# x read feature-major, and twelve pairs' C11 products first, the early ones on inputs that are not normalized

## The chip, the cores and the metric

One Trainium2 chip, one of its cores. The metric is the device time of one execution in microseconds; the median of three runs of the kernel before is 1115.58 us (1115.43 to 1116.25).

## The reference

A two-layer decoder trunk over 1024 tokens of width 1024, all in float32. Layer 0: `y = rms_norm(x)`, one projection `proj = y @ w_in` to 6144 columns, split into u (pooled with trailing windows 2, 4, 8, 16, then mixed by `w_pool`), gate_b, gate_c and h_c (the gated width-3 convolution `gate_b * conv(gate_c * h_c)`), and z (2048 columns, SiLU gate over both), then `@ w_out` and the residual. Layer 1: `rms_norm`, a q/k/v/gate projection, sliding-window attention with sinks and partial rotary, gate, `@ w_o`, residual. A final rms_norm.

```python
def rms_norm(x, g):
    x32 = x.astype(jnp.float32)
    r = x32 * lax.rsqrt(jnp.mean(x32 * x32, axis=-1, keepdims=True) + NORM_EPS)
    return (r * g.astype(jnp.float32)).astype(x.dtype)
```

The factor of a token is the rsqrt; `g` is a factor of the feature.

## The kernel before

Everything lies feature-major: 128 features on the partitions, 512 tokens (half of the sequence, s = 0 or 1) along a row. Float32 accuracy comes from splitting each operand into a high part, which ScalarE rounds to fp32r (`cast`, L181 or L469), and a low part, which VectorE gets by subtracting the high part from the source (`low`, L182 or L472). A product of two operands is then three matmuls (high x high, high x low, low x high).

The projections use Strassen's scheme in Winograd's form on 2 x 2 blocks: weights are taken in pairs of 128-column blocks, the 1024 features in two halves of 512 and the tokens in two halves. A pair needs seven products instead of eight, each of four feature slices times three matmuls of 512 columns (12 matmuls, L388). Their names are those of the weight side: A11 and A12 (a first block's feature halves, times B11 and B21, which are the normalized inputs of the first 512 tokens), S2, S1, S3, A22 and S4 (sums of weight blocks, times T2, T1, T3, T4 and B22, which are sums or parts of the normalized inputs). The sum of A11 B11 and A12 B21 is the output block C11. Layer 0 has 24 pairs: four U (pooled channels), eight CH (gate_c and h_c), eight BZ (gate_b and z), four Z (z of the pooled half), worked off as U, CH, BZ, Z, CH, BZ for each quarter of the channels; layer 1 has 9.

`Strassen.prods` is the list of all products in the order in which their weights are prepared. `prepare_to(n)` splits the weights of the next products (a cast on ScalarE, a low part on VectorE, three VectorE sums ahead of S2) and issues later loads from SyncE's queue; `lead` is 3, so weights are ready three products ahead. Weight tiles come from the pool `W` with 9 slots of 4 KB. `go_ahead` runs the A11 and A12 products of the first AHEAD = 6 pairs before any pair is worked off as a whole: B11 and B21 are all that they need, and while TensorE does them, VectorE and ScalarE make T1 to T4 and B22 (the `combine`, `cast` and `low` steps handed to it). After each product ScalarE copies the PSUM bank out, and a store puts it into `c_dram`; `pair` loads it back later and does the other five products (`pair` does all seven for the other pairs, L409).

The opening (L533 to L602) stands in an order written out by hand on TensorE, ScalarE, VectorE and SyncE (`order()`). x is read token-major, eight tiles of 128 tokens x 1024 features (`load_x`, 512 KB each). ScalarE squares a tile and sums along the row (`square`, L542); after four tiles `rsqrt_mean` (L129) gives the tokens' factors; VectorE multiplies by the factor and by `g` (`normed`, L545); TensorE transposes 128 x 128 blocks (`turned`, L553), and the results are copied out to Y. Then B11 and B21 are split, the first product starts, four products run, the second half is transposed, and eight more follow. Warm-up matmuls (L529) run in the first microseconds and between the transposes. From `ordered.close()` on only TensorE's order is the program's; the other engines are ordered by the scheduler.

Layer 1 uses the same class with all nine pairs ahead (AHEAD1 = 9). Its column sums (`col_sums`, L176) and its factor rows (`diag_r` L153 to L164, `spread_r` L166: a diagonal of the factors, multiplied by ones, gives a row of factors on all partitions) are the functions that the change also uses in layer 0.

Of the kernel before, what the change touches and what calls it, by code (L numbers as in the profile page):

```python
# [18 lines left out]
P = 128  # L19
# [17 lines left out]
AHEAD = 6  # L37
AHEAD1 = 9
# [35 lines left out]
def trunk(ctx, tc, x, xT, g1, pos, cols, w_in, w_pool, w_out, w_l1, b_kv, sinks, w_o, g_fin, out):  # L74
# [10 lines left out]
    c_dram = tc.dram_tile([AHEAD, 2, P, HALF], F32, name="c_dram")  # L85
    o_dram = tc.dram_tile([16, 2, P, HALF], F32, name="o_dram")
    c1_dram = tc.dram_tile([AHEAD1, 2, P, HALF], F32, name="c1_dram")
# [224 lines left out]
    class Strassen:  # L312


        def __init__(self, src, pairs, first, c_dram, bank, s1, u2, keep0):
            self.src, self.pairs, self.first, self.c_dram = src, pairs, first, c_dram
            self.bank, self.s1, self.u2, self.keep0 = bank, s1, u2, keep0
            pr = [(i, n) for j in range(0, first, 2) for n in ("A11", "A12")
                  for i in range(j, min(j + 2, first))]
            pr += [(i, n) for i in range(first) for n in order_ if n not in ("A11", "A12")]  # L320
            pr += [(i, n) for i in range(first, len(pairs)) for n in order_]
            if keep0 is False:
                for i in range(first - 1):
                    pr.remove((i, "S4"))
                    pr.insert(pr.index((i + 1, "S2")) + 1, (i, "S4"))
# [3 lines left out]
            self.kept, self.c_bank, self.ahead = {}, {}, {}  # L329
            self.store, self.rest, self.defer = nc.sync.dma_start, None, False  # L330
# [5 lines left out]
        def load_for(self, n):  # L336

            if n < len(self.prods):
                i, what = self.prods[n]
                if what == "A11":  # L340
                    self.load_w(i, 0)
                if i < self.first and what == "S2":
                    self.load_w(i, 0)
                    self.load_w(i, 1)

        def prepare_to(self, n):
            while self.prepared < min(n, len(self.prods)):
# [5 lines left out]
                a11, a12 = wraw[i, 0][:, 0:4], wraw[i, 0][:, 4:8]  # L353
                if not ahead:
                    if (i, 1) not in wraw:
# [10 lines left out]
                src = a11 if what in ("A11", "S2") else a12 if what in ("A12", "S4") else \  # L366
# [24 lines left out]
        def go_ahead(self, *steps):  # L391
# [984 lines left out]
```

## Time and profile before

| what | value |
|---|---|
| median of three runs | 1115.58 us |
| the profiled execution | 1114.73 us, span 1112.9 us |
| TensorE busy | 1060.9 us, 95% of the span, 4780 matmuls |
| VectorE busy | 816.7 us, 73% |
| ScalarE busy | 502.6 us, 45% |
| granted TensorE clock, mean | 0.987 |
| moved by DMA | 143.7 MB, mean 129 GB/s |

Busy time is time in which an engine has an instruction under way. A matmul that is part of a stream is listed at some 395 ns, though the next begins 233 ns behind it, so starts are what is to be compared. [...]

### The profile page before, as it was taken

The page shows a single profiled execution, that of the slowest core. Times are in us where ns is not written, and L with a number is a line of the kernel's source. Part 1 is how long each engine was busy: PE and PEld are TensorE (multiplying, and loading weights), DVE is VectorE, ACT ScalarE, POOL GpSimd, SP SyncE. Part 2 cuts the span into 40 slices and gives each one's busy share as a digit, 9 for nine tenths or more (in the row PEclk, how much of TensorE's full clock was granted, in tenths as well). Part 3 has the DMA queues.
Part 4 walks back from the last instruction along what each step waited for, and adds up shares of the span by engine and source line. Part 5 has one row for each costly group of instructions (what it writes and reads, how often), then busy time and mean ns, then how long its engine had stood idle before and what let it go on. Part 6 is the DMA issues. An engine that isn't in the chain of part 4 may idle for free. (4 is left out here: it accounts for less than half of the span.)

```text
span 1112.9 us, 13964 instructions
## 1 busy us (share of the span) xinstructions
PE 1060.9 (95%) x4780; PEld 860.5 (77%) x4780; DVE 816.7 (73%) x1544; ACT 502.6 (45%) x1007; POOL 124.1 (11%) x204
## 2 busy tenths in 40 slices
PE   3999999999999999999999999999989988999997
PEld 3778788888888888888788888877867776788886
DVE  4699979967697578955744784397688777888874
ACT  4753342333224231432633653264244698766652
POOL 0000000000000000000000000003120021455552
PEclk9999999999999999999999999999989999999999
DMA  5343331131211221224544553355348836756451
GB/s 209 107 170 102 133 129 57 67 113 39 76 57 67 95 76 38 95 86 154 204 172 142 199 174 119 122 180 180 114 160 274 276 115 178 209 115 124 97 103 39
DMA packets 108136, 143.71 MB, mean 129 GB/s; under 512 B 39584, under 2 KB 64288, under 8 KB 108064
## 3 DMA queue, kind: packets, MB, share of 16 engines
q1 hardware_dynamic: 99856, 126.03, 36.0%
q10 hardware_dynamic: 8208, 16.78, 4.1%
q8 instruction: 38, 0.62, 0.2%
q14 instruction: 34, 0.28, 0.1%
HBM read 106.35 MB, written 36.44 MB: 128 GB/s over the span
## 5 line engine op out<-in xcount | busy, mean ns | idle before, releaser
L181 ACT CAST W<-W 128x512 fp32r<-128x512 f32 (+1 forms) x234 | 156.4, 679 | 284.6 <-DVE W L363 101.3
L182 DVE TENSOR_TENSOR W<-W 128x512 fp32r<-128x512 f32 (+1 forms) x234 | 175.4, 759 | 110.8 <-ACT W L181 69.7
L388 PE MATMUL b<-U,W 128*128 128x512 f32 x432 | 110.9, 410 | 5.1 <-DVE t L433 2.2
L388 PEld LDWEIGHTS b<-U,W 128*128 128x128 f32 x432 | 82.6, 196 | 24.3 <-ACT W L181 2.7
L388 PE MATMUL b<-B11h,W 128*128 128x512 f32 x264 | 88.9, 401 | 2.7 <-ACT W L181 1.8
L388 PE MATMUL b<-B22h,W 128*128 128x512 f32 x264 | 88.5, 396 | 2.1 <-DVE t L442 2.0
L388 PE MATMUL b<-B21h,W 128*128 128x512 f32 x264 | 87.6, 396 | 1.3 <-ACT W L400 1.3
L388 PE MATMUL b<-T2h,W 128*128 128x512 f32 x192 | 65.5, 402 | 1.9 <-ACT W L181 1.9
L388 PE MATMUL b<-T3h,W 128*128 128x512 f32 x192 | 64.2, 395 | 0.0
L388 PE MATMUL b<-T1h,W 128*128 128x512 f32 x192 | 64.2, 395 | 0.0
L388 PE MATMUL b<-T4h,W 128*128 128x512 f32 x192 | 63.2, 390 | 0.0
L388 PEld LDWEIGHTS b<-B11h,W 128*128 128x128 f32 x264 | 50.3, 191 | 15.7 <-ACT W L181 2.3
L388 PEld LDWEIGHTS b<-B22h,W 128*128 128x128 f32 x264 | 49.5, 188 | 15.2 <-ACT t L987 2.0
L388 PEld LDWEIGHTS b<-B21h,W 128*128 128x128 f32 x264 | 49.6, 188 | 13.8 <-ACT W L400 2.1
L1102 ACT ACTIVATE pt<-psB,smax 128x128 f32<-128x128 f32 x128 | 45.7, 366 | 20.8 <-DVE smax L1100 20.2
L828 PE MATMUL psD<-U,W 128*128 128x512 f32 x128 | 51.3, 401 | 2.6 <-DVE U L182 2.6
L388 PE MATMUL b<-B11l,W 128*128 128x512 f32 x132 | 52.8, 400 | 0.8 <-DVE B11l L472 0.8
L388 PE MATMUL b<-B21l,W 128*128 128x512 f32 x132 | 52.1, 395 | 0.0
L388 PE MATMUL b<-B22l,W 128*128 128x512 f32 x132 | 52.1, 394 | 0.0
L1225 PE MATMUL b<-U,aH 128*128 128x512 f32 (+1 forms) x128 | 49.8, 389 | 1.6 <-DVE U L182 1.6
L829 PE MATMUL psD<-U,W 128*128 128x512 f32 x128 | 51.1, 400 | 0.0
L827 PE MATMUL psD<-U,W 128*128 128x512 f32 x128 | 51.1, 399 | 0.0
(286 smaller groups left out, 2476.2 us busy)
## 6 DMA issues: line engine op xcount, KB each, us to landing
W<-w_in SPq DMA_DIRECT2D x54, 512.0 KB, 3.3
W<-w_out SPq DMA_DIRECT2D x32, 512.0 KB, 3.4
W<-w_l SPq DMA_DIRECT2D x27, 512.0 KB, 3.9
t<-q_dram SPq DMA_DIRECT2D x32, 256.0 KB, 4.3
o_dram<-t SPq DMA_DIRECT2D x30, 256.0 KB, 2.0
t<-c_dram SPq DMA_DIRECT2D x28, 256.0 KB, 3.8
c_dram<-W ACTq DMA_DIRECT2D x18, 256.0 KB, 3.2
T<-xT SPq DMA_DIRECT2D x16, 256.0 KB, 4.2
```

The costliest lines, as they stand in the source:

```text
L181: nc.scalar.copy(out=dst_h, in_=src)
L182: sub(out=dst_l, in0=src, in1=dst_h.bitcast(F32), op=ALU.subtract)
L388: mm(dst, lhsT=w[:, hw, k], rhs=x[hx][:, k], start=start and k + n == 0, stop=k == 3 and n == 2, skip_group_check=not start)
L827: mm(dst, lhsT=w[k][0], rhs=oHL[f][0], start=(f == 0), stop=False)
L828: mm(dst, lhsT=w[k][0], rhs=oHL[f][1], start=False, stop=False)
L829: mm(dst, lhsT=w[k][1], rhs=oHL[f][0], start=False, stop=(f == 15))
L1102: act(out=res[g][:, 2 * i2 + i, :], in_=bv[:, i, P:256], func=AF.Exp, scale=0.125, bias=smax[:, at + i:at + i + 1], accum_out=den[:, at + ...
L1225: mm(o, lhsT=a[0][:, kk, :], rhs=woL[8 * n + k][:, c], start=False, stop=False)
```

## The change

x is no longer read token-major: `xT` (feature-major) is loaded in sixteen slices of 128 features x 512 tokens (256 KB) straight into Y, and the tile of `g` on all partitions, the 64 transposes and their copies out of PSUM go. Each slice of the first half is multiplied by `g` (a factor per partition here) and split into G11 and G21, operands that lack the tokens' factors (they use the space of T1 and B22). The first twelve products, A11 of six pairs and then A12 of the same six, run on G11 and G21. Since a token is a column of the product, its factor is applied afterwards: VectorE multiplies the PSUM bank by a row of factors on its way to SBUF (`scaled`), in place of ScalarE's copy, and SyncE stores it to `c_dram`. The sums of squares come from squares of the slices (VectorE for the first half, ScalarE for the second) and small matmuls with two columns of ones (`stat`, four per slice); `root` and `spread` make the rows. Then x itself is normalized in Y (`normed`), B11 and B21 are split as before, and twelve more products, of six further pairs, run on them while T1 to T4 and B22 are made. So twelve pairs instead of six are ahead: the eight BZ and the four Z (`early`). They were U0, CH0, BZ0, CH1, BZ1 and Z0.

The weights of the products ahead are loaded in halves of 256 KB, just the part that is needed, and `load_ahead` keeps `look` of them on their way. Copies of products ahead lie in tiles of their own. In `pair`, an early pair does S3 in front of S1. Layer 1 takes the same class, with the same nine pairs in the same groups as before.

The calls of the schedule are written several to a line here.

```diff
-AHEAD = 6
-AHEAD1 = 9
+GROUPS = (6, 2, 2, 2)
+GROUPS1 = (2, 2, 2, 2, 1)
...
-        def __init__(self, src, pairs, first, c_dram, bank, s1, u2, keep0):
+        def __init__(self, src, pairs, early, groups, c_dram, bank, s1, u2, defer):
+            first = len(early)
             self.src, self.pairs, self.first, self.c_dram = src, pairs, first, c_dram
-            self.bank, self.s1, self.u2, self.keep0 = bank, s1, u2, keep0
-            pr = [(i, n) for j in range(0, first, 2) for n in ("A11", "A12")
-                  for i in range(j, min(j + 2, first))]
-            pr += [(i, n) for i in range(first) for n in order_ if n not in ("A11", "A12")]
-            pr += [(i, n) for i in range(first, len(pairs)) for n in order_]
-            if keep0 is False:
-                for i in range(first - 1):
+            self.bank, self.s1, self.u2, self.early = bank, s1, u2, early
+            pr, j = [], 0
+            for n_ in groups:
+                pr += [(i, n) for n in ("A11", "A12") for i in early[j:j + n_]]
+                j += n_
+            pr += [(i, n) for i in range(len(pairs))
+                   for n in (("S2", "S3", "S1", "A22", "S4") if i in early else order_)]
+            if defer:
+                for i in range(len(pairs) - 1):
                     pr.remove((i, "S4"))
                     pr.insert(pr.index((i + 1, "S2")) + 1, (i, "S4"))
...
-                if what == "A11":
+                if n < 2 * self.first:
+                    k = 4 * int(what == "A12")
+                    self.part[i, what] = W([P, 4, P])
+                    nc.sync.dma_start(out=self.part[i, what],
+                                      in_=self.src[self.pairs[i][0]][:, k:k + 4])
+                elif what == "A11":
                     self.load_w(i, 0)
-                if i < self.first and what == "S2":
+                if i in self.early and what == "S2":
                     self.load_w(i, 0)
                     self.load_w(i, 1)
+
+        def load_ahead(self, n):
+            while len(self.loaded) < min(n, 2 * self.first):
+                self.loaded.append(self.load_for(len(self.loaded)))
 
...
+                src = self.part.pop((i, what)) if ahead else a11 if what in ("A11", "S2") else a12 if what in ("A12", "S4") else \
...
-                    if at_ + 2 < 2 * self.first:
-                        self.load_for(at_ + 2)
-                    elif at_ + 1 == 2 * self.first:
+                    self.load_ahead(at_ + 1 + self.look)
+                    if at_ + 1 == 2 * self.first:
                         self.load_for(2 * self.first)
                 elif i + 1 < len(self.pairs):
-                    if what == "A12" or i < self.first and what == "S3":
+                    if what == "A12" or i in self.early and what == "S1":
                         self.load_w(i + 1, 0)
                     if what == "A22":
...
+        def go_ahead(self, *steps, names=("B11", "B21"), row=None, late=None):
...
-                    self.c_bank[i], self.kept[i] = self.bank(), W([P, 2, HALF])
-                self.product(self.c_bank[i], i, what, ("B11", "B21")[j], j == 0)
-                t = self.kept[i][:, j]
-                nc.scalar.copy(out=t, in_=self.c_bank[i])
-                if i or not self.keep0:
-                    self.store(out=self.c_dram[i, j], in_=t)
-                    t = self.c_dram[i, j]
-                self.ahead[i, j] = t
-                self.prepare_to(min(len(self.ahead) + LEAD, 2 * self.first + 3))
+                    self.c_bank[i] = self.bank()
+                self.ahead[i, j] = None
+                self.product(self.c_bank[i], i, what, names[j], j == 0)
+
+                def rest(i=i, j=j, row=row):
+                    t = self.out()
+                    if row is None and late is None:
+                        nc.scalar.copy(out=t, in_=self.c_bank[i])
+                    else:
+                        tt(out=t, in0=self.c_bank[i], in1=row(), op=ALU.mult)
+                    self.ahead[i, j] = at_ = self.c_dram[self.early.index(i), j]
+                    self.store(out=at_, in_=t)
+
+                if late is None:
+                    rest()
+                else:
+                    late.append(rest)
+                self.prepare_to(min(len(self.ahead) + self.lead, 2 * self.first + 3))
...
+            if i in self.early:
+                p1, c = t3(), t3()
+                for j, t in enumerate((p1, c)):
+                    nc.sync.dma_start(out=t, in_=self.ahead[i, j])
                 c11(c)
             else:
                 p1 = t3()
@@ -433,15 +453,21 @@
             tt(out=u2_, in0=b2, in1=p1, op=ALU.add)
             self.finish_pair()
             run(0)
+            if i in self.early:
+                b2 = bank()
+                product(b2, i, "S3", "T3")
+                tt(out=p1, in0=b2, in1=u2_, op=ALU.add)
+                run(1)
             b3 = bank()
             product(b3, i, "S1", "T1")
-            run(1)
-            b2 = bank()
-            product(b2, i, "S3", "T3")
-            tt(out=p1, in0=b2, in1=u2_, op=ALU.add)
+            if i not in self.early:
+                run(1)
+                b2 = bank()
+                product(b2, i, "S3", "T3")
+                tt(out=p1, in0=b2, in1=u2_, op=ALU.add)
             tt(out=o22, in0=b3, in1=p1, op=ALU.add)
             run(2)
-            if i >= self.first:
+            if i not in self.early:
                 product(b1, i, "A12", "B21", False)
                 c11(b1)
...
+    st0 = Strassen(w_in, pairs, [BZ[j] for j in range(8)] + [Z[g] for g in range(4)], GROUPS,
+                   c_dram, bank,
...
+    ops["G11"], ops["G21"] = ops["T1"], ops["B22"]
...
+    def xt(s, k):
+        return Y[f"{k // 4 + 1}{s + 1}"][:, k % 4]
+    def load_x(s, *ks):
+        for k in ks:
+            nc.sync.dma_start(out=xt(s, k), in_=xT[k * P:(k + 1) * P, hs(s)])
+    def operand(k):
+        h, lo = (t[:, k % 4] for t in ops[("G11", "G21")[k // 4]])
+        act(out=h, in_=xt(0, k), func=AF.Copy, scale=col(C_G1, k))
+        stt(out=lo, in0=xt(0, k), scalar=col(C_G1, k), in1=h.bitcast(F32), op0=ALU.mult,
+            op1=ALU.subtract)
+    sq, sums, rows = {}, {}, {}
+    def square(s, k):
+        sq[s, k] = xp.tile([P, HALF], F32, name="sq", bufs=4)
+        if s:
+            act(out=sq[s, k], in_=xt(s, k), func=AF.Square)
+        else:
+            tt(out=sq[s, k], in0=xt(s, k), in1=xt(s, k), op=ALU.mult)
+    def stat(s, k):
+        if k == 0:
+            sums[s] = bank()
+        for b in range(4):
+            c = 8 * k + 2 * b
+            mm(sums[s][:, c:c + 2], lhsT=sq[s, k][:, b * P:(b + 1) * P], rhs=ones[:, 0:2],
+               start=True, stop=True)
+    def root(s):
+        r = rcol0[:, 4 * s:4 * s + 4]
+        nc.vector.tensor_reduce(out=r, in_=sums[s][:, 0:64].rearrange(
+            "p (k b x) -> p b k x", b=4, x=2)[:, :, :, 0], axis=AX.X, op=ALU.add)
+        rsqrt_mean(const, r, r, 4)
+        sums[s] = diag_r(rcol0, s)
+    def spread(s):
+        rows[s] = xp.tile([P, HALF], F32, name=f"row{s}")
+        nc.scalar.copy(out=rows[s], in_=spread_r(sums[s], bank()))
+    def normed(s, k):
+        x_ = xt(s, k)
+        stt(out=x_, in0=x_, scalar=col(C_G1, k), in1=rows[s], op0=ALU.mult, op1=ALU.mult)
+    late = []
+    def products(n, f=None):
+        go_ahead(*[[]] * n, names=("G11", "G21"), row=lambda: rows[0], late=late)
+    def scaled(n):
+        for _ in range(n):
+            late.pop(0)()
...
+    nc.sync.dma_start(out=colt, in_=cols)
+    st0.load_ahead(1)
+    load_x(0, 0, 1, 2, 3)
+    st0.load_ahead(2)
+    load_x(0, 4)
+    st0.load_ahead(3)
+    load_x(0, 5)
+    load_x(0, 6, 7)
     st0.prepare_to(1)
+    for k in range(8):
+        operand(k)
+        square(0, k)
+        if k == 1:
+            warm_up(4)
+        if k in (3, 5, 6):
+            st0.prepare_to({3: 2, 5: 3, 6: 4}[k])
+        if k in (4, 6):
+            load_x(1, *range(2 * k - 8, 2 * k - 4))
+
+    def stats(s, *ks):
+        return [lambda k=k: stat(s, k) for k in ks]
+    def sq_stat(*ks):
+        return [lambda k=k, f=f: f(1, k) for f in (square, stat) for k in ks]
+    def nr(s, *ks):
+        return [lambda k=k: normed(s, k) for k in ks]
+    prep = st0.prepare_to; st0.out = lambda: xp.tile([P, HALF], F32, name="out", bufs=3)
+    products(1); run(stats(0, *range(8))); prep(3); root(0); products(1); spread(0)
+    products(1); run(sq_stat(0, 1, 2, 3)); prep(4); scaled(2); prep(5); run(nr(0, 0, 1))
+    scaled(1); products(1); run(sq_stat(4, 5, 6, 7)); prep(6); run(nr(0, 2, 3)); scaled(1)
+    products(1); prep(7); run(nr(0, 4, 5)); products(1); prep(8); scaled(2); run(nr(0, 6, 7))
+    products(1); prep(9); run(cast(ops["B11"], b11, HK) + low(ops["B11"], b11, HK))
+    products(1); prep(10); root(1); products(1); spread(1); prep(11)
+    run(cast(ops["B21"], b21, HK) + low(ops["B21"], b21, HK)); products(1); scaled(2)
+    prep(12); run(nr(1, 0, 4, 1)); products(1); scaled(1); prep(13); run(nr(1, 5, 2))
+    products(1); scaled(1); prep(14); run(nr(1, 6, 3, 7)); scaled(2); st0.lead = LEAD
+    st0.out = lambda: W([P, HALF])
...
+    go_ahead(combine(b12, b22, b12, ALU.subtract, HK),
+             combine(b11, b12, b11, ALU.add, HK),
+             cast(ops["T2"], b11, HK) + low(ops["T2"], b11, HK),
+             cast(ops["T3"], b12, HK) + low(ops["T3"], b12, HK),
              combine(b12, b22, b11, ALU.subtract, HK) + cast(ops["B22"], b22, HK),
+             cast(ops["T1"], b12, HK) + low(ops["T1"], b12, HK),
+             combine(b21, b21, b11, ALU.subtract, HK),
+             cast(ops["T4"], b21, HK) + low(ops["B22"], b22, HK),
+             low(ops["T4"], b21, HK), [], [], [])
```

## Rows read from the trace of the kernel before

**Rows 1.** Busy time by stage of the opening (start:end, length, busy us and instructions of each engine, granted TensorE clock, DMA share, GB/s).
```profile
0.00:26.49 26.49, 10.09 (x56) 8.41 (x56) 11.17 (x24) 10.14 (x17) 2.06 (x27) 1.00 0.56 219
26.49:46.10 19.61, 17.00 (x80) 13.48 (x81) 15.08 (x25) 14.51 (x26) 0.00 (x0) 0.91 0.28 98
46.10:85.00 38.90, 36.87 (x152) 28.99 (x151) 33.74 (x40) 23.11 (x36) 0.00 (x0) 0.96 0.44 154
85.00:130.00 45.00, 44.84 (x194) 36.02 (x193) 42.56 (x68) 13.78 (x24) 0.22 (x2) 1.00 0.38 129
130.00:200.00 70.00, 70.00 (x303) 56.47 (x302) 61.81 (x147) 23.34 (x40) 0.33 (x3) 1.00 0.25 82
```
**Rows 2.** Line L388, the products' matmuls by operand (duration ns min/median/max, first to last start).
```profile
L388 PE MATMUL b<-B11h,W x264: 390/395/645, 26.5 to 765.6; 128*128 128x512 f32 x132
L388 PE MATMUL b<-B22h,W x264: 390/395/475, 83.9 to 929.9; 128*128 128x512 f32 x132
L388 PE MATMUL b<-T2h,W x192: 390/394/767, 70.8 to 516.5; 128*128 128x512 f32 x192
L388 PE MATMUL b<-T1h,W x192: 390/393/405, 75.3 to 519.3; 128*128 128x512 f32 x192
L388 PE MATMUL b<-T3h,W x192: 390/394/404, 78.1 to 522.1; 128*128 128x512 f32 x192
```
**Rows 3.** VectorE in order of time (start, length of the run, instruction, xcount).
```profile
13.82 0.16 DVE L140 TENSOR_SCALAR rs_v<-ss 128x4 f32<-128x4 f32 x1
...
15.79 0.16 DVE L151 SCALAR_TENSOR_TENSOR rcol<-rs_a,rs_y 128x4 f32<-128x4 f32 x1
...
38.12 4.87 DVE L545 SCALAR_TENSOR_TENSOR x<-x,rcol,W 128x1024 f32<-128x1024 f32 x4
42.91 1.89 DVE L182 TENSOR_TENSOR W<-W 128x512 fp32r<-128x512 f32 x3
...
53.03 2.36 DVE L476 TENSOR_TENSOR y<-y,y 128x1024 f32<-128x1024 f32 x2
...
640.39 0.69 DVE L162 TENSOR_TENSOR W<-ident,rl 128x512 fp32r<-128x512 f32 x1
```
**Rows 4.** ScalarE in order of time (in brackets: idle before, and its releaser).
```profile
4.20 1.06 ACT L542 ACTIVATE W<-T 128x1024 bf16<-128x1024 f32 x1 [1.90 <-DMA T<-x]
...
31.75 1.66 ACT L181 CAST W<-W 128x512 fp32r<-128x512 f32 x3
...
43.91 4.01 ACT L554 COPY y<-b 128x512 f32<-128x512 f32 x8
```
**Rows 5.** Two lines: a sum out of PSUM, a copy with a column factor.
```profile
L433 DVE TENSOR_TENSOR t<-b,t x32: 672/683/693, 93.3 to 916.5; 128x512 f32<-128x512 f32 x32
L844 ACT ACTIVATE y<-t,colt x16: 716/722/726, 547.2 to 716.1; 128x512 f32<-128x512 f32 x16
```
**Rows 6.** TensorE in order of time: transposes, and column sums (L176).
```profile
17.42 1.94 PE L553 MATMUL b<-ident,T 128*128 128x128 f32 x8 [14.41 <-DVE T L545]
...
42.70 3.66 PE L553 MATMUL b<-ident,x 128*128 128x128 f32 x32
...
635.49 0.95 PE L176 MATMUL psB<-ones,acc 128*128 128x2 f32 x8
```
**Rows 7.** Busy time by stage again: single microseconds, stretches with many loads, layer 1.
```profile
34.00:35.00 1.00, 1.00 (x4) 0.80 (x3) 0.29 (x1) 1.00 (x3) 0.00 (x0) 0.50 0.09 20
69.00:70.00 1.00, 0.00 (x0) 0.00 (x0) 0.90 (x2) 0.00 (x0) 0.00 (x0) 1.00 0.00 0
72.00:73.00 1.00, 1.00 (x4) 0.82 (x3) 1.00 (x2) 1.00 (x2) 0.00 (x0) 0.50 0.00 0
7.00:16.00 9.00, 0.00 (x0) 0.00 (x0) 2.41 (x13) 2.92 (x5) 0.00 (x0) 1.00 1.02 412
524.00:530.00 6.00, 6.00 (x28) 4.89 (x27) 1.91 (x3) 1.82 (x4) 0.00 (x0) 1.00 1.02 390
820.00:830.00 10.00, 7.84 (x30) 5.92 (x28) 8.84 (x18) 5.08 (x11) 4.06 (x12) 0.83 0.57 195
```

More of the change, by code (lines that the diff above doesn't have):

```diff
@@ L328, in __init__ @@
             self.prepared, self.lead, self.made = 0, 0, {}
-            self.kept, self.c_bank, self.ahead = {}, {}, {}
-            self.store, self.rest, self.defer = nc.sync.dma_start, None, False
+            self.c_bank, self.ahead = {}, {}
+            self.store, self.rest, self.defer = nc.sync.dma_start, None, defer
+            self.loaded, self.part, self.look, self.out = [], {}, 3, lambda: W([P, HALF])
         def load_w(self, i, j):
@@ L580, in trunk @@
-    nc.sync.dma_start(out=colt, in_=cols)
-    run(cast(ops["B11"], b11, HK))
-    square(4)
-    run(cast(ops["B21"], b21, HK))
-    run(low(ops["B11"], b11, HK) + low(ops["B21"], b21, HK))
-    square(5)
-    go_ahead([lambda: square(6), lambda: square(7),
-              lambda: rsqrt_mean(const, rcol0[:, 4:8], ss[:, 4:8], 4)]
-             + [lambda b=b: normed(b) for b in range(4, 8)], [], [], [])
-    for b in range(4, 8):
-        turned(b)
+    def xt(s, k):
+        return Y[f"{k // 4 + 1}{s + 1}"][:, k % 4]
@@ new lines, in sq_stat @@
+    def sq_stat(*ks):
+        return [lambda k=k, f=f: f(1, k) for f in (square, stat) for k in ks]
+    def nr(s, *ks):
+        return [lambda k=k: normed(s, k) for k in ks]
+    prep = st0.prepare_to
+    st0.out = lambda: xp.tile([P, HALF], F32, name="out", bufs=3)
+    products(1)
+    run(stats(0, *range(8)))
+    prep(3)
+    root(0)
+    products(1)
+    spread(0)
+    products(1)
+    run(sq_stat(0, 1, 2, 3))
+    prep(4)
+    scaled(2)
+    prep(5)
+    run(nr(0, 0, 1))
+    scaled(1)
@@ new lines, in trunk @@
+    products(1)
+    run(sq_stat(4, 5, 6, 7))
+    prep(6)
+    run(nr(0, 2, 3))
+    scaled(1)
+    products(1)
+    prep(7)
+    run(nr(0, 4, 5))
+    products(1)
+    prep(8)
+    scaled(2)
+    run(nr(0, 6, 7))
+    products(1)
+    prep(9)
+    run(cast(ops["B11"], b11, HK) + low(ops["B11"], b11, HK))
+    products(1)
+    prep(10)
+    root(1)
+    products(1)
+    spread(1)
+    prep(11)
+    run(cast(ops["B21"], b21, HK) + low(ops["B21"], b21, HK))
+    products(1)
+    scaled(2)
+    prep(12)
@@ L591, in trunk @@
+    run(nr(1, 0, 4, 1))
+    products(1)
+    scaled(1)
+    prep(13)
+    run(nr(1, 5, 2))
+    products(1)
+    scaled(1)
+    prep(14)
+    run(nr(1, 6, 3, 7))
+    scaled(2)
+    st0.lead = LEAD
+    st0.out = lambda: W([P, HALF])
     xp.release()
@@ L858, in trunk @@
     st1 = Strassen(w_l1, [(8, 9)] + [(2 * i, 2 * i + 1) for i in (0, 1, 2, 3, 5, 6, 7, 8)],
[L859 to L860 removed]
+                   list(range(9)), GROUPS1, c1_dram, lambda: pools["ps"].tile([P, HALF], F32, name="b"),
+                   lambda i: keep.tile([P, 4, P], F32, name="S1", bufs=1), lambda i: t3(), True)
+    st1.look, st1.lead = 2, LEAD
     st1.ops.update(ops1)
[L862 to L863 removed]
+    st1.load_ahead(2)
     st1.prepare_to(2)
```

75 lines of the change are left out of this document (6 added, 69 removed).

## The prediction

> **What bounds the kernel now.** I read the page's busy shares first (TensorE is busy for 95% of the span), then the busy time by stage, then TensorE's waits and instructions in order of time. The stages show where the other 5% lie [rows 1]: from 130 to 200 us TensorE has no gap at all, from 85 to 130 us 0.16 us, but the first 85 us hold 16.4 us, 2.6 us and 2.0 us of idle time, and what is busy before 26.5 us is warm-up and transposes. So inside layer 0 only the opening can give time; afterwards the kernel goes as fast as TensorE multiplies.
>
> I measure the opening by its lag: the time that has passed, less 2.8 us for each product of 12 matmuls that is done. 2.8 us is the step from the first T1 matmul (75.3) to the first T3 matmul (78.1) [rows 2]. The first product starts at 26.5, the first S2 product (T2) at 70.8 with 12 products done: lag 70.8 - 33.5 = 37.3 us. At 83.9 (B22) there are 16 done: lag 39.3 us, and it stays there. [...] The change has to be judged by the lag that it leaves.
>
> **The change, part by part.** The number of products stays 24 x 7; the change takes out 64 transposes, the copies behind them and the wait for normalized x, and adds work on VectorE and small matmuls. I walk the four queues with cadences (start to start) from the trace. VectorE: 0.60 for 512 columns (three in 1.89, one lasts 0.69), 1.14 for 1024 (two in 2.36), 0.66 for 512 columns with a column factor (0.60 and the 0.06 by which 1024 columns with a factor, 1.20 from four in 4.87, are above 1.14), 2.1 for the rsqrt chain (13.82 to 15.95), 1.3 for the two diagonal tiles [rows 3]. ScalarE: 0.52 for a cast, 0.49 for a copy out of PSUM [rows 4], 0.72 for one with a column factor [rows 5].
>
> Loads. Before, the first 512 KB of x are used at 4.20 [rows 4]; the first 256 KB of the first weights and of x are the same bytes, so x slice 0 is there at about 4.1. Later slices come every 0.65 us: 256 KB at the 412 GB/s of the stretch from 7 to 16 us; rows of 2 KB, as the new loads have them, ran at 390 GB/s from 524 to 530 [rows 7]. If each cost half as much again (0.97 us), VectorE's pace of 1.26 us a slice would still cover it. [...]
>
> First half of x. VectorE does per slice a low part (0.66) and a square (0.60), and three weight lows between: from 4.1 it ends the eighth square at 16.8. Product 1 runs at that pace (three matmuls a slice) from 5.7 to 11. Then TensorE's queue holds 32 small matmuls for the sums of squares, in front of product 2. Four of that kind took 0.95 us (eight instructions) [rows 6], so a slice costs 0.95, and the last is done at 18.5. The trace shows them only once, at the full clock and in a busy stretch; the nearest rows for their cost on either side are eight transposes, which took 1.94 us at the start and 0.91 us (32 in 3.66) later [rows 6]. I take 0.95 and keep 1.75 as the upper end; the lower end is nothing, if they slip in beside the weight loads of the products.
>
> Factors. Reduction, rsqrt chain and diagonals: 4.1 us, VectorE at 22.6; spread matmuls and ScalarE's copy: row 0 at 24.2. Product 2 lies inside. I let it run at half rate for a while (+1.7 us), since what goes before it is thin; that shifts the end by 0.5.
>
> Rest of the first twelve. Behind product 3 (26.3) TensorE has four slices of sums for the second half (3.8 us), product 4, four more (3.8), products 5 and 6: 42.3. VectorE waits in this stretch: 1.9 for the last sums, 1.7 for row 0, 1.6 for ScalarE, which squares first and casts the next weights behind, 1.4 and 5.7 for products. From 42.4 VectorE sets the time: scaling of products 6 to 12 (PSUM to SBUF, 0.60 each; 683 ns against 0.69 us from SBUF [rows 3, 5]), normalizing, lows of B11 and B21, second factors, weight lows: 23 us of work and 2.1 us of waiting for row 1: 67.4. TensorE ends product 12 at 61.1 and waits there in pieces. The twelve scalings, which ScalarE did as copies (0.49 each [rows 4]), are 7.2 us of VectorE's time. [...]
>
> Second twelve. Nine steps of two 1024-column instructions and one weight low: 9 x 2.9 us, then S2's sums; products take 2.8. TensorE follows VectorE closely; S2 of pair 0 starts at 98.5, with 25 products done (pair 0 has its A11 product first now): lag 98.5 - 69.8 = 28.7 us. SyncE's loads of later weights stand behind stores that wait for the scaling; they are issued three products ahead (8.4 us), above the 4 us within which the first x tile was there, so they cost nothing unless a slot comes late: then up to 3 us.
>
> Sum: 39.3 - 28.7 = 10.6 us. I give back 1.7 us for one more fall of the clock, as at 72 to 73, behind one of the gaps: 8.9 us. The profiled execution took 1114.7 us (span 1112.9): 1105.8. It lies 0.85 below the median of 1115.6, so about **1107 us** on that scale.
>
> At nothing I cost: twelve more loads and stores of partial products and the weights read twice (DMA busy 0.25 to 0.44 in layer 0 [rows 1]); BZ and Z as early pairs (VectorE work per pair some 11 us for BZ beside 14 us of TensorE; if t3 tiles run out, a wait of 2 us in each of three Z pairs); S3 ahead of S1 and half-size weight loads in layer 1, where TensorE loses 2.2 us of idle time and 1.7 us of clock in a stretch like 820 to 830 [rows 7] because VectorE is late: that can shift by 2 us either way.
>
> **The rivals.** (1) Dearer sums in the first half: they run at half rate, 1.75 a slice. They start at 11 and end at 25.0 instead of 18.5; everything behind shifts by 6.4 us: gain 4.2 less 1.7: about 1113, or 1111 without the fall. For it: the transposes at 17.4, which took twice the later time though TensorE was busy [rows 6]. Against: product 1 keeps TensorE full for 5 us just before.
> (2) Slower than before: the sums stay at half rate in both halves, and products 2, 4 and 5 start at half rate behind them. The walk then reaches S2 6.4 + 6.4 + 3.4 = 16.2 us later, lag 44.9: 5.6 us over before, about 1121. It decides where a slice costs over 1.45 us in both halves. For it: at 34 to 35 the clock is at 0.50 after a stretch in which TensorE did little [rows 7], and the trace has no such matmuls in a row. Against: the 32 transposes in a row at 42.7 ran at full rate [rows 6].
> (3) Cheaper sums: they hide beside weight loads, VectorE alone bounds: lag 20.9, gain 18.4 less 1.7, about 1098 to 1099. Against: the one row for them shows instructions 0.12 us apart.
> (4) The opening gains as forecast but Z pairs, the W slots or layer 1 give it back (three waits of 2 us and a fall of the clock each): 1113 to 1118.
>
> **How the numbers follow.** Forecast 0.45 (1103 to 1110), rival 1 0.19, rival 2 0.14, rival 3 0.12, rival 4 0.10. 0.2% is 2.2 us, about what a measurement can tell from no change: faster means below 1113.4. The forecast, rival 3 and the better part of rival 1 lie there (0.45 + 0.12 + 0.13 = 0.70), the rest of rival 1 and nine tenths of rival 4 within (0.15), rival 2 and what is left above (0.15). The range goes from the edge of rival 3 to a little short of rival 2: 1098 to 1119.
>
> **What would show it.** The first product at 5 to 6 us, the eighth slice of sums done near 18.5, row 0 near 24, product 12 near 61, pair 0's T2 at 96 to 101, and no TensorE gap from there to layer 0's end. T2 above 109 means that there is no gain. Sums at 0.2 us apart per instruction, or a granted clock of 0.50 between 12 and 40 us, speak for rivals 1 and 2; VectorE with hardly a wait between 17 and 42 for rival 3. Wrong altogether would be a start that waits for the loads, or new gaps behind 130 us.

## The result: 0.8% slower

| | kernel before | changed kernel |
|---|---|---|
| median (8 runs each, side by side) | 1115.45 us | 1125.25 us |
| lowest to highest | 1115.09 to 1116.25 | 1119.16 to 1127.83 |
| ratio to before | | 1.0083 (95%: 1.0064 to 1.0101) |
| profiled execution, its span | 1114.73, 1112.9 | 1126.95, 1125.2 |
| TensorE / VectorE / ScalarE busy | 1060.9 / 816.7 / 502.6 | 1083.6 / 834.2 / 490.3 |
| granted clock, mean | 0.987 | 0.975 |

The forecast of 1107 us and its sign were wrong, and 1125 lies outside its range. The profiled execution lies 1.7 us above its median, so differences read from its trace add up to 12.3 us and not to 9.8. I read the changed kernel's profile in the order in which the prediction walked it: stages, landmarks, then the queues.

Busy time by stage of the changed kernel, in the columns of [rows 1], and below it three shorter stretches:
```profile
0.00:26.49 26.49, 23.26 (x100) 19.16 (x101) 16.86 (x39) 9.22 (x14) 1.94 (x27) 0.81 0.65 230
26.49:46.10 19.61, 19.61 (x99) 17.23 (x98) 9.14 (x14) 7.34 (x13) 0.00 (x0) 0.74 0.31 107
46.10:85.00 38.90, 37.49 (x157) 28.76 (x156) 31.36 (x53) 13.57 (x21) 0.00 (x0) 1.00 0.42 144
85.00:130.00 45.00, 43.09 (x179) 34.31 (x178) 37.21 (x48) 23.94 (x39) 0.00 (x0) 0.96 0.37 130
...
12.00:14.00 2.00, 2.00 (x20) 2.00 (x20) 1.78 (x3) 1.76 (x4) 0.00 (x0) 1.00 1.05 402
14.00:16.00 2.00, 2.00 (x17) 2.00 (x16) 2.00 (x5) 0.14 (x1) 0.00 (x0) 0.79 1.06 389
16.00:25.00 9.00, 9.00 (x37) 8.42 (x38) 4.64 (x18) 0.00 (x0) 0.00 (x0) 0.50 0.37 137
```
The change did what it says: TensorE is busy from 6 us on, 23.3 us of the first 26.5 where it was 10.1. But in the second line it is busy without a gap while its granted clock (as a share of the full one) is 0.74, and from 16 to 25 it is busy all the time at 0.50. Busy time counts small matmuls and half rate like full work, so the column that looked like the gain is not one. The landmarks say what was done by when (line L400, the products by operand; product 1 reads T1h, product 7 B22h, product 13 B11h, and pair 0's S2 product T2h):
```profile
L400 PE MATMUL b<-T1h,W x240: 391/394/792, 6.0 to 533.3; 128*128 128x512 f32 x120
L400 PE MATMUL b<-B22h,W x312: 388/396/632, 50.0 to 945.8; 128*128 128x512 f32 x156
L400 PE MATMUL b<-B11h,W x216: 388/394/505, 68.9 to 772.8; 128*128 128x512 f32 x108
L400 PE MATMUL b<-T2h,W x192: 391/394/632, 110.2 to 527.7; 128*128 128x512 f32 x192
```
T2h first at 110.2 with 25 products done is a lag of 110.2 - 69.8 = 40.4 us, against 39.3 before: the opening gave nothing, by the prediction's own sign ("T2 above 109"). Between 11 and 50 us the cause is in TensorE's rows: the small matmuls of the sums of squares (L592), and the spreading of a row (L169). The rows of L400 around them belong to products 1 and 2.
```profile
9.61 0.63 PE L400 MATMUL b<-T1l,W 128*128 128x512 f32 x1
...
10.89 0.63 PE L400 MATMUL b<-T1l,W 128*128 128x512 f32 x1
...
11.74 10.55 PE L592 MATMUL b<-ones,sq 128*128 128x2 f32 x64
...
22.73 0.63 PE L400 MATMUL b<-T1l,W 128*128 128x512 f32 x1
...
24.01 0.63 PE L400 MATMUL b<-T1l,W 128*128 128x512 f32 x1
...
26.50 0.62 PE L169 MATMUL b<-W,onesr 128*128 128x512 f32 x2
...
29.77 4.59 PE L592 MATMUL b<-ones,sq 128*128 128x2 f32 x32
...
39.29 3.93 PE L592 MATMUL b<-ones,sq 128*128 128x2 f32 x32
```
From 22.73 to 24.01 product 2 makes three matmuls, 0.43 us each, at a granted clock of 0.50; in a stream at 1.00 the step is 0.233 us. Product 1 has the same step of 0.43 us from 9.61 to 10.89, so it ran at half rate too, though the windows show 1.00 there. The trace's records of the clock begin at 11.7 us (at 23.1 in the kernel before), and the 1.00 shown ahead of them is not a reading; where they begin earlier, in the run with products ahead below, product 1 shows 0.50 from 8 to 11 us.

VectorE in the same stretch (in brackets idle time and releaser):
```profile
17.73 0.68 DVE L584 TENSOR_TENSOR sq<-y 128x512 f32<-128x512 f32 x1
...
22.33 0.19 DVE L597 TENSOR_REDUCE rcol<-b 128x4 f32<-128x32 f32 x1 [3.91 <-PE b L592]
```
VectorE has its last square at 18.4 and waits 3.9 us for TensorE's sums: TensorE is the bound here, and it is the sums that it does.

The rest of the loss is behind the opening. The sum into the first w_out tile (L952) starts at 553.9, 7.4 us after before's 546.5; the last at 723.3, 7.9 after 715.4; the end is 12.3 us later. Since the lag at T2 is only 1.1 us larger, some 6 us go in layer 0's pair stage and 4 in layer 1. The sums into the w_out tiles, before (L843) and changed (the other tile of L952 stands under Layer 1 below):
```profile
L843 DVE TENSOR_TENSOR t<-psD,T x8: 683/684/693, 546.5 to 704.2; 128x512 f32<-128x512 f32 x8
L843 DVE TENSOR_TENSOR t<-psA,T x8: 682/684/693, 558.6 to 715.4; 128x512 f32<-128x512 f32 x8
```
```profile
L952 DVE TENSOR_TENSOR t<-psD,T x8: 683/688/696, 553.9 to 712.1; 128x512 f32<-128x512 f32 x8
```
TensorE's waits in 250 to 290, and in 830 to 850, of the changed kernel (releaser: total us, times, longest):
```profile
PE b L400 <- DVE cos L245: 2.0, 1, 2.0
...
PE b L400 <- DVE t L453: 5.2, 1, 5.2
```
The first is the table of cosines for layer 1's rotary step, which VectorE computes between the pairs; the half rate behind that gap shows in the stages (columns as above):
```profile
260.00:270.00 10.00, 8.04 (x31) 6.17 (x30) 9.32 (x31) 4.45 (x9) 0.11 (x1) 0.89 0.30 102
270.00:280.00 10.00, 10.00 (x42) 8.02 (x41) 9.21 (x15) 2.53 (x6) 0.22 (x2) 0.94 0.37 131
...
130.00:538.00 408.00, 404.07 (x1724) 323.83 (x1723) 328.05 (x566) 126.61 (x215) 1.57 (x14) 1.00 0.30 102
```
In the pair stage as a whole TensorE now idles for 3.9 us. In the kernel before, whose pair stage ended at 531, it had no gap there:
```profile
130.00:531.00 401.00, 401.00 (x1726) 323.46 (x1724) 303.97 (x523) 130.19 (x220) 1.34 (x12) 1.00 0.24 83
```

### The profile page after: what moved, and what is told of

It reads as the page before. It is cut to its first block, busy times and chain, and to the rows that moved or that the text cites. A ratio compares the mean times of both kernels' runs of the same rounds, so it can differ in the third digit from the quotient of the medians.

```text
span 1125.2 us, 14271 instructions
## 1 busy us (share of the span) xinstructions
PE 1083.6 (96%) x4836; PEld 876.0 (78%) x4836; DVE 834.2 (74%) x1586; ACT 490.3 (44%) x989; POOL 125.0 (11%) x204
## 5 line engine op out<-in xcount | busy, mean ns | idle before, releaser
L400 PE MATMUL b<-U,W 128*128 128x512 f32 x432 | 112.2, 414 | 5.5 <-DVE t L453 5.2
L400 PE MATMUL b<-B22h,W 128*128 128x512 f32 x312 | 105.6, 401 | 6.2 <-DVE t L468 3.9
L400 PEld LDWEIGHTS b<-U,W 128*128 128x128 f32 x432 | 83.7, 198 | 24.7 <-DVE t L453 5.4
L400 PE MATMUL b<-T1h,W 128*128 128x512 f32 x240 | 86.0, 421 | 2.1 <-ACT T1h L573 2.1
L400 PE MATMUL b<-B21h,W 128*128 128x512 f32 x216 | 74.2, 410 | 4.8 <-ACT W L417 4.3
L400 PEld LDWEIGHTS b<-B22h,W 128*128 128x128 f32 x312 | 59.1, 190 | 23.6 <-issue 6.7
L400 PE MATMUL b<-B11h,W 128*128 128x512 f32 x216 | 71.3, 396 | 0.1
L400 PE MATMUL b<-T2h,W 128*128 128x512 f32 x192 | 64.5, 397 | 0.0
L400 PE MATMUL b<-T3h,W 128*128 128x512 f32 x192 | 64.3, 395 | 0.0
L400 PE MATMUL b<-T4h,W 128*128 128x512 f32 x192 | 63.4, 391 | 0.0
L400 PE MATMUL b<-B22l,W 128*128 128x512 f32 x156 | 62.3, 399 | 0.0
L400 PEld LDWEIGHTS b<-T1h,W 128*128 128x128 f32 x240 | 48.8, 203 | 14.0 <-ACT T1h L573 2.6
L400 PEld LDWEIGHTS b<-B21h,W 128*128 128x128 f32 x216 | 41.9, 194 | 16.2 <-ACT W L417 5.2
L936 PE MATMUL psA<-U,W 128*128 128x512 f32 x128 | 50.8, 397 | 0.0
L938 PE MATMUL psA<-U,W 128*128 128x512 f32 x128 | 50.7, 396 | 0.0
```

The source lines that it names most:

```text
L400: mm(dst, lhsT=w[:, hw, k], rhs=x[hx][:, k], start=start and k + n == 0, stop=k == 3 and n == 2, skip_group_check=not start)
L936: mm(dst, lhsT=w[k][0], rhs=oHL[f][0], start=(f == 0), stop=False)
L938: mm(dst, lhsT=w[k][1], rhs=oHL[f][0], start=False, stop=(f == 15))
```

## The experiments

Three losses, so three theories. O: the opening's gain is eaten by TensorE, by the small sums and the half clock. Q: layer 0's pair stage loses at the tables on VectorE. L: layer 1 loses by its new order and halved loads. The rivals: V, VectorE bounds the opening whatever the sums cost; D, the losses behind the opening fall out by chance. The expectations use letters of their own beside these: P (the tables stand in the wrong place), C (the clock makes the sums dear), S (the sums are dear whatever the clock does). Ratios are to the kernel before, run on the same chip.

**Sums by wide matmuls.** The squares are written as fp32r and multiplied by a matrix of ones, 512 columns at a time; four small sums per half remain.
```
-        for b in range(4):
-            c = 8 * k + 2 * b
-            mm(sums[s][:, c:c + 2], lhsT=sq[s, k][:, b * P:(b + 1) * P], rhs=ones[:, 0:2], ...)
+        mm(sums[s], lhsT=onesr, rhs=sq[s, k], start=(k == 0), stop=(k == 7))
```


> The changed kernel, only its column sums done otherwise: the squares are written as fp32r, eight matmuls of 128x512 against a matrix of ones gather them in one bank, ScalarE copies the bank, and four small sums turn it into columns; order of the work unchanged. Theory O (the 10.55 us and 8.52 us of the small sums on TensorE, and the half clock that they leave behind, are what the opening lost): the sums of the first half end at 19 instead of 22.2 (the last square ends at 18.4), those of the second half take 2.5 instead of 8.5, products 4 and 5 run at 2.8 instead of 4.8 and 3.3; first S2 product of pair 0 at 100 to 102 instead of 110.2; time 1114 to 1118, 8 to 11 below the changed kernel's 1125. Rival V (VectorE and ScalarE bound the opening anyway): the S2 product stays at 108 to 111 and the time at 1123 to 1127.

Measured: 1115.15 us, ratio 0.9992 (0.9979 to 1.0006), 10 us below the changed kernel. TensorE's sums (L592, L599) in order of time, and T2h:
```profile
11.58 1.07 PE L592 MATMUL b<-sq,onesr 128*128 128x512 f32 x4
...
18.47 0.80 PE L592 MATMUL b<-sq,onesr 128*128 128x512 f32 x1 [1.37 <-DVE sq L586]
20.04 1.84 PE L599 MATMUL b<-part,sq 128*128 128x2 f32 x8 [0.77 <-ACT sq L597]
...
30.39 1.09 PE L592 MATMUL b<-sq,onesr 128*128 128x512 f32 x4
...
34.10 1.09 PE L592 MATMUL b<-sq,onesr 128*128 128x512 f32 x4
...
L402 PE MATMUL b<-T2h,W x192: 390/393/404, 102.1 to 516.5; 128*128 128x512 f32 x192
```
The second half's sums fell from 8.5 to 2.2 us (and 0.95 for the four small ones at 46.2), T2 comes 8.1 us earlier, and TensorE's clock was 1.00 from 30 to 40. Theory O holds and V is out; the intervals of the two ratios lie apart. How much of the 8.1 us is work of the small sums and how much the clock is not taken apart. One forecast failed: the first half's sums ended at 21.9, not at 19. TensorE waits there for the squares (1.37 us ahead of the last one), its clock was 0.59 on average from 16 to 22, and the eight instructions of the four small sums took 1.84 us.

**Fillers.** Two bf16 matmuls of 256 columns behind each slice's sums.
```
+        for _ in range(2):
+            mm(sums[s][:, 256:512], lhsT=wu[:, 0:P], rhs=wu, start=True, stop=True)
```


> The changed kernel with two bf16 matmuls of 256 columns added behind the four small sums of every slice, 32 in all; nothing else changed. Theory C (the small sums are dear because TensorE's clock falls to half among them, and the filling matmuls hold it): granted clock 1.00 over 16 to 50, the sums of the first half end by 20 in spite of the added work, products 2, 4 and 5 take 2.8 each, time 1119 to 1122. Theory S (the sums cost their own issue and weight loads, whatever the clock does): the fillers only add 32 times 0.11 to 0.23 us to TensorE's queue, the sums still end at 22 to 26, time 1126 to 1130.

Measured: 1125.56 us, 1.0094 (1.0081 to 1.0108); T2 at 114.1. The sums of one slice each, in order of time:
```profile
13.21 0.95 PE L592 MATMUL b<-ones,sq 128*128 128x2 f32 x8
...
15.27 1.31 PE L592 MATMUL b<-ones,sq 128*128 128x2 f32 x8
...
16.81 1.71 PE L592 MATMUL b<-ones,sq 128*128 128x2 f32 x8
```
The fillers did not hold the clock (it was 0.50 from 16 to 24, so theory C as I had it fell; the time lies just under what theory S gave), but they separate the slices, and the price can be read: 0.95 us at the full clock, as forecast, and 1.71 us, 1.8 times as much, once the clock is at 0.50. So S is not right either: what was wrong in the prediction was the clock, not the count.

**Products ahead of the row.** Small sums kept; products 2 and 3 go ahead of them or between them, and product 4 and the second half's squares ahead of the row.
```
-    products(1)
-    run(stats(0, *range(8)))
+    products(2)
+    run(stats(0, *range(6)))
+    products(1)
+    run(stats(0, 6, 7))
+    root(0)
+    products(1)
...
```


> The changed kernel with its small sums kept, but products 2 and 3 put ahead of them or between them, product 4 before the row is spread, and the second half's squares taken before that. TensorE does the same work; theory O (TensorE is what the opening waits for, and its half clock behind the sums is the rest): only what stood idle and the half clock come back, first S2 product of pair 0 at 104 to 108 instead of 110.2, time 1119 to 1123. Rival V (the row's later arrival, by some 3 us, holds up VectorE, which then ends the phase later): S2 at 110 or later, time 1125 to 1128.

Measured: 1121.51 us, 1.0047 (1.0032 to 1.0061), T2 at 106.7. 3.7 us came back, though the first row was copied out at 34.8 instead of 27.2: TensorE's queue, not VectorE, was what the opening waited for. The order also shows what the clock does behind a product at the full rate. Product 2 now ends at 14.6 with steps of 0.23 us, and the sums begin right behind it; the second half's first four slices stand between products 4 and 5 (TensorE's rows, then busy time by stage):
```profile
14.64 7.29 PE L592 MATMUL b<-ones,sq 128*128 128x2 f32 x48
...
30.58 3.63 PE L592 MATMUL b<-ones,sq 128*128 128x2 f32 x32
```
```profile
8.00:11.00 3.00, 2.79 (x7) 1.68 (x6) 3.00 (x6) 1.66 (x3) 0.00 (x0) 0.50 0.97 346
14.00:17.00 3.00, 3.00 (x26) 2.87 (x25) 1.37 (x3) 1.07 (x2) 0.00 (x0) 1.00 1.05 387
18.00:24.00 6.00, 6.00 (x24) 5.59 (x25) 3.32 (x6) 1.26 (x2) 0.00 (x0) 0.50 0.37 127
...
30.00:34.00 4.00, 4.00 (x36) 3.86 (x34) 2.35 (x7) 0.00 (x0) 0.00 (x0) 1.00 0.01 2
35.00:38.00 3.00, 3.00 (x9) 2.32 (x8) 2.04 (x4) 3.00 (x7) 0.00 (x0) 0.50 0.00 0
```
The clock still falls among the sums, and behind the 3.63 us of the second block product 5 runs at half rate, without idle time in TensorE's records.

**The tables, later in layer 0.** The same instructions after the second gated group.
```
-        if g == 0:
-            gated(g, src)
-            with tc.tile_pool(name="rope", bufs=1) as pr, tc.issue_after(spilled[-1].ins):
+        if g == 0:
+            gated(g, src)
+        if g == 1:
+            with tc.tile_pool(name="rope", bufs=1) as pr, tc.issue_after(spilled[-1].ins):
```


> The changed kernel, only the rope tables computed after the second gated group instead of the first (the same instructions, a pair stage later). Theory P (the 2.0 us gap at 264 and the half clock behind it, some 4.3 us in all, come from the rope tables' instructions on VectorE falling where pairs have five products): they go, the first w_out matmul comes 4 us earlier (535), time 1121. Rival Q (VectorE has no room for the tables beside any two such pairs): the gap of 2 us and the fall of the clock appear between 310 and 400 instead, time 1125.

Measured: 1127.09 us, 1.0109 (1.0090 to 1.0127). TensorE has no gap from 260 to 280 any more (busy for all 20 us at 1.00), and this one instead (columns as above; then its longest wait there):
```profile
350.00:360.00 10.00, 9.63 (x42) 7.53 (x41) 10.00 (x25) 2.77 (x5) 0.11 (x1) 1.00 0.45 139
...
370.00:380.00 10.00, 7.70 (x27) 5.85 (x26) 8.98 (x29) 5.42 (x10) 0.00 (x0) 0.83 0.19 64
```
```profile
PE b L400 <- DVE sin L243: 2.3, 1, 2.3
```
The gap follows the tables, with its half clock. Theory P is out: the place within the layer is not at fault, and beside these pairs VectorE, busy for all of 350 to 360, has no room for them.

**The tables, in the w_out stage.** There VectorE had time: in the changed kernel it is busy for 16.7 of the 40 us from 580 to 620.
```
+            added = tt(out=h1, in0=dst, in1=xin, op=ALU.add)
+            if s == 0 and m == 1:
+                with tc.tile_pool(name="rope", bufs=1) as pr, tc.issue_after(added.ins):
+                    rope_tables(pr)
+                    small_loads()
```


> The changed kernel, only the rope tables moved behind the second output tile of the w_out stage, where VectorE was busy 8 of 20 us. Theory Q' (in layer 0 VectorE has no room for their 25 us beside pairs of five products; moving them within the layer did not help, moving them out of it does): the gap at 264 and the half clock behind it go, first w_out result 4 us earlier, time 1120 to 1122. Rival: the stage gives the 4 us back in layer 1, or the tables are late there: 1124 to 1127.

Measured: 1122.33 us, 1.0057 (1.0041 to 1.0073), 2.9 us below the changed kernel by the medians. The stretch of the gap, and the stretch that took the tables in:
```profile
260.00:270.00 10.00, 10.00 (x45) 8.08 (x44) 9.91 (x17) 5.22 (x9) 0.11 (x1) 1.00 0.35 125
...
580.00:620.00 40.00, 40.00 (x173) 32.20 (x172) 22.50 (x55) 14.27 (x19) 0.00 (x0) 1.00 0.42 140
```
Theory Q holds: beside w_out, VectorE has them within 22.5 of 40 us and TensorE does not notice. That the gap goes is shown, and the first w_out sum comes 3.8 us earlier (550.1 against 553.9). What it is worth in the end is less sure: the ratio's interval overlaps with the changed kernel's, and in the trace layer 1 takes 1.8 us longer (403.7 against 401.9 from the last w_out sum to the end).

**Layer 1.** Four kernels: the changed one with the order back, with the loads and copies back, with both back, and the kernel before with the order alone. One line of the order's edit; the rest of it and the edit of the loads are left out here:
```
-                   for n in (("S2", "S3", "S1", "A22", "S4") if i in early else order_)]
+                   for n in (("S2", "S1", "S3", "A22", "S4") if i in early and defer else ...)]
```


> The changed kernel, only layer 1's pairs (and the order of their weights) back to S2, S1, S3. Theory L (the new order costs layer 1 the 7 us by which its last pair's S2 falls further behind than its first w_out matmul did): last S2 sum at 925 instead of 931.7, waits of TensorE in layer 1 down by 5, time 1119. Rival D (layer 1's waits are those of loads from DRAM and of the half clock that fall out differently in each run): time 1123 to 1127.

> The kernel before with one part of the change alone: in the early pairs of both layers S3 comes before S1. Theory L: 4 to 7 us slower than before in layer 1, 1120 to 1122. Rival D: within 1 us of before, 1115 to 1117. If the order is a gain, as the change would have it: 1112 to 1114.

> The changed kernel with layer 1's Strassen work as in the kernel before: order S2, S1, S3, whole 512 KB loads of each A11's tile, both products of a pair copied into one buffer. Theory L' (the two edits together, the order and the halved loads, cost layer 1 the 3 to 5 us by which its time from the last w_out result to the end is longer: 401.9 against 397.5): that stretch at 397 to 399, time 1121 to 1123. Rival D (it is the phase in which the loads and the half clock happen to fall): 400 to 402 and 1124 to 1127.

> The changed kernel; in layer 1 only the loads and copies are as before (whole 512 KB tiles, both products of a pair in one buffer), the new order S2, S3, S1 stays. With the order undone alone the time was 1126.85, with order and loads undone 1121.88. If the loads (twice as many transfers on SP's queue and two buffers' slots where there was one) are what costs layer 1: 1120 to 1123, and 397 to 400 from the last w_out result to the end. If the two only cost together (each alone leaves the other's waits): 1124 to 1127.

| kernel | median us | ratio (95%) | from the last w_out sum to the end, us |
|---|---|---|---|
| before | 1115.45 | | 1112.9 - 715.4 = 397.5 |
| changed | 1125.25 | 1.0083 (1.0064 to 1.0101) | 1125.2 - 723.3 = 401.9 |
| changed, order back | 1126.85 | 1.0097 (1.0081 to 1.0112) | 1125.1 - 724.5 = 400.6 |
| changed, loads back | 1124.12 | 1.0082 (1.0068 to 1.0096) | 1119.4 - 722.5 = 396.9 |
| changed, both back | 1121.88 | 1.0061 (1.0046 to 1.0077) | 1119.3 - 721.6 = 397.7 |
| before, order alone (both layers) | 1117.78 | 1.0027 (1.0015 to 1.0039) | 1115.0 - 714.2 = 400.8 |

The last w_out sums of the changed kernel (L952) and of the one with both back (L956), first to last start:
```profile
L952 DVE TENSOR_TENSOR t<-psA,T x8: 683/684/692, 566.1 to 723.3; 128x512 f32<-128x512 f32 x8
```
```profile
L956 DVE TENSOR_TENSOR t<-psA,T x8: 683/684/692, 564.4 to 721.6; 128x512 f32<-128x512 f32 x8
```
Both edits together cost layer 1 3.4 us by the medians and 4.2 by the stretch; the forecast had them at nothing. On these runs alone that is not clear of the noise (the intervals of "changed" and "both back" overlap, and the profile of "both back" is of the fastest of its six runs); the kernel with four edits below makes it clear. The order alone makes the kernel before slower (by 0.27%), though by less than theory L had it, yet taking it back alone gives the changed kernel nothing. The profile of "loads back" shows the short stretch, but it is of the fastest of its five runs, and its median gained only 1.1: the time is what the expectation gave for "only together", the stretch nearer to what it gave for the loads. How the 3.4 us divide stays open.

**Three edits, four edits.** Wide sums, products ahead of the row, tables in the w_out stage; then layer 1 as before too.

> Three edits together on the changed kernel: the sums by matmuls of 512 columns, products 2 to 4 ahead of the row, the rope tables in the w_out stage. By theory O and Q': S2 of pair 0 at 95 to 98, no gap in 200 to 300, time 1104 to 1108, faster than both kernels. If VectorE bounds the opening once the sums are cheap: S2 at 100 to 102 and time 1110 to 1112. If layer 1 gives back what comes earlier: 1113 to 1116.

> The kernel of the three edits (sums by 512 columns, products ahead of the row, rope tables in the w_out stage), and layer 1 as before. By theory L' 1102 to 1105; by rival D 1106 to 1108.

Measured: 1107.10 us, 0.9924 (0.9908 to 0.9939), T2 at 98.4; and 1100.61 us, 0.9872 (0.9852 to 0.9891), T2 at 95.1. Both beat both kernels. The fourth edit gives 6.5 us by the medians, with intervals apart, and 6.0 by the stretch from the last w_out sum to the end (395.4 against 401.4). That is more than theory L' had; rival D is out, and that layer 1's edits cost time is shown. How much is less sure: the profiles are of the second slowest of six runs and of the fastest of five, and T2 is 3.3 us earlier in the second although both kernels have the same opening. Stages of the one with four edits:
```profile
0.00:26.49 26.49, 20.52 (x79) 13.99 (x80) 16.16 (x38) 12.45 (x20) 1.98 (x28) 0.94 0.74 254
26.49:46.10 19.61, 17.18 (x78) 13.15 (x76) 18.07 (x38) 7.85 (x13) 0.00 (x0) 1.00 0.43 148
46.10:85.00 38.90, 36.57 (x151) 28.07 (x152) 35.85 (x45) 22.73 (x34) 0.00 (x0) 1.00 0.53 171
```
TensorE is less busy in the first 85 us than in the changed kernel (74.3 against 80.4 us) and 15 us ahead of it at T2: it does less that is not a product, and at a clock of 0.94, then 1.00. From 26 to 46 VectorE is now the fuller queue (18.1 of 19.6).

**Which pairs first.** The three edits, but the first 12 pairs in order.
```
-    st0 = Strassen(w_in, pairs, [BZ[j] for j in range(8)] + [Z[g] for g in range(4)], GROUPS,
+    st0 = Strassen(w_in, pairs, list(range(12)), GROUPS,
```


> The kernel of the three edits, but the 12 early pairs are the first 12 in order (two U, four CH, four BZ, two Z) instead of the eight BZ and four Z. TensorE's work is the same. Theory V (beside a pair of five products, 14 us of TensorE, VectorE has 15 adds, combinations and splits of 0.69 us, 10.3 us, and what the pair itself needs: 2.8 us for BZ, 4 for CH, 10 for U; in a row such pairs are bound by VectorE): gaps of TensorE in 100 to 300, 6 to 12 us in all with the half clock behind them, first w_out result at 543 to 549 instead of 537.4, time 1113 to 1119. Rival: the choice does not matter since VectorE runs ahead on the later pairs: 1106 to 1109.

Measured: 1110.04 us, 0.9954 (0.9937 to 0.9972), 2.9 above the chosen pairs by the medians (the intervals overlap) and just above what the rival gave, with one long gap of TensorE (its wait, and the stage):
```profile
PE b L402 <- ACT W L419: 3.8, 1, 3.8
```
```profile
85.00:100.00 15.00, 11.22 (x42) 8.72 (x41) 10.52 (x13) 6.33 (x13) 0.00 (x0) 0.89 0.65 221
100.00:300.00 200.00, 199.33 (x858) 160.70 (x858) 168.02 (x256) 62.84 (x106) 0.90 (x8) 1.00 0.36 120
```
VectorE does not bind in a row of such pairs (0.7 us of gaps from 100 to 300): my figure of 6 to 12 us fell. The choice is worth at most some 3 us. By the traces 2.1 us are lost when the pairs begin (T2 at 97.7 with 24 products done, lag 30.7 against 28.6), where TensorE waits for ScalarE's copies into W tiles, and 1.0 us at the first w_out sum (538.4 against 537.4).

## Why the prediction was wrong, point by point

- What bounds the kernel (TensorE, and inside layer 0 only the opening can give time): right for before. "Afterwards the kernel goes as fast as TensorE multiplies" held for before's pairs, and I carried it over to pairs of five products.
- Loads and start: right. First product 5.98 (5.7), product 1 done at 11.7 (11), DMA at 402 GB/s from 12 to 14. But product 1 ran at half rate (0.43 us a matmul), which the prediction took for a full TensorE; half rate fits the slow transposes at 17.4 [rows 6] as well.
- Sums of the first half, the step that failed: done at 22.3 instead of 18.5. The price per slice of 0.95 us was right at the full clock; the clock left it after 15 us. On average a slice cost 10.55 / 8 = 1.32 us, and 8.52 / 8 = 1.07 in the second half, where I had 0.95. Behind them product 2 took 4.3 us from start to start (22.2 to 26.5), much as I had allowed (2.8 and 1.7); product 4 took 5.1 (34.2 to 39.3) and products 5 and 6 together 7.0 (43.1 to 50.0), instead of 2.8 each. Of the 7.7 us by which product 7 came late (50.0 against 42.3), 3.5 are there when product 3 ends (29.8 against 26.3), 0.6 come from the second sums (start to start), 2.3 from product 4, 1.4 from products 5 and 6.
- The clock at 1.7 us for product 2 and one more fall of 1.7: the mis-sized term. Up to 50 us the half clock is in all four parts of those 7.7 us. My rival 2 had the mechanism (sums at half rate in both halves, products 2, 4 and 5 behind them) and put its point at 1.45 us a slice in both halves. The clock came back between the bursts (1.00 from 25.5 to 32 and from 46 to 85), so the lag stopped at 40.4, between rival 1 and rival 2's 44.9. Against it I had set that 32 transposes ran at the full clock [rows 6]. Both kinds fill TensorE's records. But behind the 32 transposes, which lasted 3.66 us, the clock stayed at 1.00 (46.4 to 48), and behind the 32 sums between products 4 and 5 in the run with products ahead, which lasted 3.63 us, it fell to 0.50.
- VectorE's pace: the eighth square ended at 18.4 (16.8), which cost nothing, since TensorE was later still. VectorE was not the bound before 50 us; with wide sums and products ahead it is busy for 18.1 of 19.6 us from 26 to 46 beside TensorE's 17.2 in the kernel with four edits (16.7 beside 18.4 in the one with three), nearer to what the forecast had.
- Second twelve: T2 41.3 us behind product 13 (37.4 forecast). A wait of 1.9 us for ScalarE's copy into a W tile and the half rate behind it (0.96 in 85 to 130) are the "up to 3 us" and the one fall of the clock that I had named.
- Edits at nothing: wrong by some 9 us in all (rival 4's place, and it came on top of the lost gain, not instead). In the pair stage I compared VectorE's 11 us for a BZ pair with TensorE's 14 and left out the tables, which before stood beside longer pairs without a gap (the cosines at 212 us); 2.9 us by the medians came back when they were moved away, the rest of that stage's 6 us (among it three waits for VectorE's sums, 1.9 us in all) was not taken apart. Layer 1: 3.4 us by the medians, 6.5 in the kernel with the other three edits, against "2 us either way".
- Cheap sums alone do not make the forecast come true: with them T2 was at 102.1 and the time 1115.15. With products ahead and the tables moved as well, T2 was at 98.4 and the time 1107.1, against a forecast of 98.5 and 1107. That it meets both so closely is in part luck, since that kernel still has layer 1's loss, which the forecast had at nothing, and an order of products that it did not have.

## What to carry over

A share of busy time near 100% does not say that TensorE works (here it was busy for all of 16 to 25 us at a clock of 0.50): read its granted clock beside it, and count products done by a landmark. Price a small operation at both clocks when it comes in rows of dozens (a slice of sums took 0.95 us at 1.00 and 1.71 at 0.50), and ask whether a wide form of it (here, ones as weights and 512 columns moving) takes less: here 8.5 us of the second half's sums became 2.2, and 0.95 for the four small ones. A stage without gaps before the change can have a margin on the second engine (here VectorE was busy for 304.0 of 401 us); if the change shortens the pairs there, add up everything else that this engine does in that stage (here the tables came on top, and TensorE idled for 3.9 us).

## What was not expected of the hardware

In a row of 64 small sums, with no idle time in the records, the granted clock fell from 1.00 (12 to 14) to 0.50 (16 to 25), and the fillers of that experiment did not prevent it. Product 1, just before, had run at half rate (steps of 0.43 us); but the clock also fell in the run with products ahead (to 0.50 from 18 to 24), where product 2 had run at the full rate (steps of 0.23 us) just before the sums. The 32 transposes of [rows 6] had left it at 1.00 (46.4 to 48). Which property of the small sums it is (two moving columns, or float32 in two instructions) no run separates, so the cause of the fall stays open.

One small fp32 sum takes two instructions of 0.119 us (0.95 / 8) at the full clock and 0.214 (1.71 / 8) at half. Both come from the run with fillers; what sets these steps, no run shows.
